# One order for the matrix memory of both sequences: scores turned on VectorE and through DRAM

## The chip, the cores and the metric

The kernel runs on one NeuronCore of a Trainium2 chip. The metric is the time of one execution on the device, in microseconds. The core has engines that each take their own instructions in order and wait for one another through semaphores: TensorE (PE, with its weight loads shown as PEld) for matmuls, VectorE (DVE), ScalarE (ACT), GpSimd (POOL) and SyncE (SP), which here only issues DMAs. An instruction that waits holds up everything behind it on its engine, and a DMA that waits holds up the DMAs issued behind it on the same queue.

## The reference

One layer of an encoder is applied to two sequences, `x_prompt` (below: the first, `s = 0`) and `x_sample` (the second, `s = 1`), of 512 tokens with 1024 channels each. Between two half-weighted feed-forward blocks stands a mix of two branches: grouped-query attention, and a bidirectional matrix memory with four heads of width 128.

```python
def encoder_layer(x, ...):
    x = x + 0.5 * swiglu(rms_norm(x, ffn1_norm), ...)
    h = rms_norm(x, mix_norm)
    proj = h @ w_in
    aq, ak, av, mq, mk, mv, gate_pre, o_pre, g_att, g_mlstm = jnp.split(proj, split_at, axis=-1)
    ...
    att = gqa_block_attention(aq, ak, av)
    mem = mlstm_bidirectional(mq, mk, mv, gate_pre, mlstm_gate_bias, o_pre, mlstm_head_norm)
    merged = jax.nn.sigmoid(g_att) * (att @ w_up_att) + jax.nn.sigmoid(g_mlstm) * (mem @ w_up_mlstm)
    x = x + merged @ w_out
    x = x + 0.5 * swiglu(rms_norm(x, ffn2_norm), ...)
    return x

def mlstm_bidirectional(q, k, v, gate_pre, ...):
    ...
    h = (h_fwd + h_bwd).transpose(0, 2, 1, 3)
    h = h * lax.rsqrt(jnp.mean(h * h, axis=-1, keepdims=True) + EPS)
    h = h.reshape(B, S, M_WIDTH) * head_norm
    return jax.nn.sigmoid(o_pre) * h

# inside one direction, for a chunk of 128 tokens:
        S_qk = jnp.einsum('bhtd,bhsd->bhts', qc, kc) * jnp.exp(D - m_t[..., None])
        num = jnp.einsum('bhts,bhse->bhte', S_qk, vc) + ...
        den = jnp.sum(S_qk, axis=-1) + ...
        h = num / jnp.maximum(jnp.abs(den), jnp.exp(-m_t))[..., None]
```

The kernel does not carry a state from chunk to chunk. For each head it forms the whole 512 x 512 matrix of decayed scores of both directions, divides its rows by the denominators, and multiplies it with the values.

## The kernel before, in words

**Precision and weights.** Every product is made of three matmuls, hi by hi, hi by lo and lo by hi, since each 32-bit operand is kept as a rounded high half and the remainder. The first sequence fetches a weight tile raw (L271, on SyncE, into a ring of four buffers with the tag `wr`), ScalarE makes the high half (L278), VectorE the low half (L279), both into a ring of four with the tag `w8`, and both halves are written to DRAM (`wpark`, L303). The second sequence reads them back from there already split (L293). `go(...)` takes units of work, each a load and a computation, and issues the load of a unit ahead of the computation of the unit before: one ahead in the first sequence, two in the second.

**The instruction order.** The text of the program gives each instruction a priority by its place; `shifted(n)` moves a piece forward or back. A scheduler at build time places instructions of each engine by their priority and by when their inputs are expected. So a change in the text's order, or of a ring from which a tile comes, can move instructions of all engines. In the stretches where `marks` is set, the matmuls at the ends of groups are pinned to the written order.

**The memory of one head** (inside `mix`):
- `mem_rows` (L1071, L1074): two DMAs on SyncE spread decay rows `ebuf` over the partitions into the tile `box` (a ring of four), and an addition with a mask makes a second copy of each. The masks of heads 1 to 3 of the first sequence are on GpSimd; all the others are on VectorE.
- `mem_head` (L1234 to L1281): four blocks of 128 rows of scores on TensorE (L1248, 12 matmuls of 512 columns); 20 exponentials on ScalarE (L1262); eight products with row sums on VectorE (L1264); the denominators (L1268 to L1270); and the two directions joined (L1275 on ScalarE, L1276 and L1278 on VectorE).
- The scores must be turned before they meet the values. The first sequence does that on TensorE in `mem_out`, with 16 transposes of 128 x 128 a head (L1307) into PSUM. The second one calls `mem_blocks` (L1283 to L1292) right behind `mem_head`: VectorE transposes within 32 x 32 blocks in eight instructions a head (L1286) into two `qt` tiles, taken from the ring `wr`; eight DMAs on SyncE (L1290) write them to `tbuf`, one of two DRAM buffers; and `mem_out` reads four blocks back by DMAs of GpSimd (L1303).
- `mem_out`: the turned block is split (L715 on ScalarE, L716 on VectorE), 12 matmuls with the values `Vm` follow (L1316), then the output gate (L1326) and the norm of the head: `block_sums` turns the squares on VectorE (L225) and reduces them (L226); `block_rstd` folds the sums with a small matmul (L232) and takes twelve operations on 128 x 16 numbers (L235 to L241); `spread_rows` (L258) and L1332 apply it, and the result is split into `mem`. Where the scores came through DRAM, the output is first copied into order by ScalarE (L1322).

**Units around it.** `mem_values` (L804, four units of 24 matmuls: `Vm`), `mem_qk` for heads 2 and 3, `att_gate`, `merge_att` (L839, L1215) and `mem_gate` are the units that give TensorE work while a head goes through ScalarE and VectorE. In the first sequence they are spread by a queue and `fill`; in the second one they are listed by hand between the heads.

The few lines that decide where the raw weights and the turned tiles live:

```python
        raw = wpool.tile(shape, F32, tag="wr", bufs=4, name=nm("wr"))                                            # L266
            q = [wpool.tile([P, 8, 4, 32], F32, tag="wr", bufs=4, name=nm("qt")) for _ in range(2)]              # L1283
```

Of the kernel before, what the change touches and what calls it, by code (L numbers as in the profile page):

```python
# [8 lines left out]
F32 = mybir.dt.float32  # L9
# [17 lines left out]
def encoder(ctx, tc, I, outs):  # L27
# [228 lines left out]
    def spread_rows(r16, R):  # L256

        nc.vector.transpose(R.rearrange("p (n j) -> p n j", j=32), r16.unsqueeze(2).to_broadcast([P, 16, 32]))  # L258
        return R
# [583 lines left out]
    FILLER = 5,3  # L843
    SOON = 7,1
    FIRST = 7,9,9,11
    EARLY = 6

    def mix(s, xh, xl, early=None, extra=None, after=None):

# [4 lines left out]
        def fill(n):  # L854
            go(*queue[:n])
            del queue[:n]
# [159 lines left out]
        def mem_qk(h, j):  # L1016
            def done(pp):
                if j == 0 and not s:
                    t = wpool.tile([P, 4, S], F32R, tag="w8", bufs=4, name=nm("qk"))
                    qks[h] = [t[:, i] for i in range(4)]  # L1020
                elif s:
                    t = mem[:, 2 + j] if h == 2 else wpool.tile([P, 2, S], F32R, tag="wr", bufs=4, name=nm("qk"))
                    qks.setdefault(h, []).extend(t[:, i] for i in range(2))
                t = pp
                if not s:
                    t = F2()
                    V_.tensor_tensor(t, pp, R[s], op=ALU.mult)
                split(t, *qks[h][2 * j:2 * j + 2])
            return win_cols((768, 1280)[j] + h * P, done)
# [264 lines left out]
        def mem_out(h, Ts):  # L1294
            moved = isinstance(Ts, int)
            vm = Vm[0]
            po = PO()
            hs_ = slice(h * P, (h + 1) * P)
            turned = []
            for j in range(4 + 1):  # L1300
                if j < 4 and moved:
                    p = F2()
                    nc.gpsimd.dma_start(p, tbuf[Ts][4 * j:4 * j + 4].rearrange("c r a x -> (c r) (a x)"))  # L1303
                elif j < 4:
                    p = PT()
                    for i in range(4):
                        nc.tensor.transpose(p[:, i * P:(i + 1) * P], Ts[i][0][:, j * P:(j + 1) * P], ident)  # L1307
                if j < 4:
                    ph, pl = T2(F32R), T2(F32R)
                    split(p, ph, pl)  # L1310
                    turned.append((j, ph, pl))
                if j >= 1:
                    t, ph, pl = turned.pop(0)
                    with shifted(15):
                        for n, (a, b) in enumerate(((0, ph), (1, ph), (0, pl))):
                            mark(nc.tensor.matmul(po, vm[:, a, t, hs_], b, start=(t == 0 and n == 0),  # L1316
                                                  stop=(t == 3 and n == 2)), True)
# [12 lines left out]
            with shifted(160):  # L1330
                Rh = spread_rows(rh, T2(F32, "f2"))
                V_.scalar_tensor_tensor(og, og, hn[:, h:h + 1], Rh, op0=ALU.mult, op1=ALU.mult)  # L1332
                split(og, mem[:, h, 0, :], mem[:, h, 1, :])

        if s:
            qk2, qk3 = [[mem_qk(h, j) for j in range(2)] for h in (2, 3)]
            ma = [merge_att(d) for d in range(KD)]
            marks[0] = True
            at = [mem_blocks(0, mem_head(0))]
            go(*mem_values(), *qk2)  # L1340
            at.append(mem_blocks(1, mem_head(1)))
            go(*qk3, ma[0], ma[1])
            mem_out(0, at[0])
            at.append(mem_blocks(2, mem_head(2)))
            go(att_gate(6), att_gate(7), ma[2], ma[3])
            mem_out(1, at[1])
            at.append(mem_blocks(3, mem_head(3)))
            go(*ma[4:])
            mem_out(2, at[2])
            go(*[mem_gate(d) for d in range(EARLY)])  # L1350
            mem_out(3, at[3])
            marks[0] = False
        for h in range(HM if not s else 0):
            Ts = mem_head(h)
            if h == 0:
                go(*mem_values())
            queue.append(merge_att(2 * h))
            if h == 0:
                queue.append(merge_att(1))
            fill(1 + s)  # L1360
            mem_out(h, Ts)
            if h + 2 < HM:
                queue.extend([att_gate(h + 6), mem_qk(h + 2, 0), mem_qk(h + 2, 1)])
            if h:
                queue.append(merge_att(2 * h + 1))
            fill(99)
# [543 lines left out]
```

## Time and profile before

| | us |
|---|---|
| runs | 2041.68, 2039.68, 2042.42 (median 2041.68) |
| profiled execution | 2039.86 |
| its span | 2038.1 |
| granted TensorE clock, mean | 0.999 |
| memory stage of the first sequence | about 800 to 980 of the span |
| memory stage of the second sequence | about 1180 to 1330 of the span |

The span is the stretch from the first to the last instruction that the profiler saw; the execution's own time is 1.8 us longer. In the lines that follow, a row of a timeline reads: start, duration, engine, line of the kernel, operation, what it writes and reads, and how many. "idle before" is the time for which that engine did nothing ahead of it, with what ended it. Matmuls are pipelined, so a single matmul's recorded duration is longer than the step from one to the next. Busy time on TensorE says that it is never without work, not that it works at its peak.

### The profile page before, as it was taken

The numbers are of one execution on the slowest core, as the hardware profiler recorded it, in microseconds if no ns is written. First come the engines' busy times: TensorE is split into PE (matmuls) and PEld (weight loads), VectorE is DVE, ScalarE is ACT, GpSimd is POOL, SyncE is SP. The second block draws the span as 40 slices with busy tenths as digits, with TensorE's granted clock in tenths as the row PEclk, the third lists the DMA queues.
The fourth block names the chain that finished last, engine by engine and source line by source line (L and its number), as shares of the span: only waits on it lengthen the run. The fifth ranks groups of instructions, "written<-read, shape, count | busy, mean of one in ns | idle before, by whom it ended". The sixth has DMA issues, their size and how long they took to land.

```text
span 2038.1 us, 26750 instructions
## 1 busy us (share of the span) xinstructions
PE 2026.7 (99%) x9249; PEld 1672.9 (82%) x9249; DVE 1580.7 (78%) x2812; ACT 912.3 (45%) x1659; POOL 101.2 (5%) x132
## 2 busy tenths in 40 slices
PE   9999999999999999999999999999999999999998
PEld 7888888888888888888888888788888888888887
DVE  8888888886797798776566767477788988786797
ACT  7644444442234577563324554235444444442224
POOL 0000000001003000100120000011000000000001
PEclk9999999999999999999999999999999999999999
DMA  9656566799766954868654367877565655699753
GB/s 320 197 167 220 178 209 189 238 334 365 268 214 224 292 176 135 274 212 294 199 186 141 110 191 241 272 231 231 180 197 175 212 171 177 205 347 345 272 197 119
DMA packets 324712, 453.78 MB, mean 223 GB/s; under 512 B 20616, under 2 KB 198880, under 8 KB 323296
## 3 DMA queue, kind: packets, MB, share of 16 engines
q1 hardware_dynamic: 321216, 441.89, 64.8%
q0 software_dynamic: 3200, 9.92, 1.5%
q8 instruction: 73, 1.20, 0.2%
q14 instruction: 63, 0.52, 0.1%
q10 hardware_dynamic: 160, 0.27, 0.0%
HBM read 288.25 MB, written 163.74 MB: 222 GB/s over the span
## 4 chain that ended last, share of the span: by engine, by line
PE 93%; DVE 3%; ACT 1%; DMA 1%; issue 1%; SPq 0%; POOL 0%; DVEq 0%; ACTq 0%; POOLq 0%
PE mm L839 13%; PE pso L374 12%; PE pst L374 12%; PE mm L374 10%; PE mm L632 9%; PE pss L374 6%; PE mm L825 5%; PE pss L632 4%; PE pst L632 4%; PE mm L804 4%; PE pso L632 3%; PE pso L1128 1%; PE pss L1101 1%; PE pst L1117 1%; PE pso L804 1%
## 5 line engine op out<-in xcount | busy, mean ns | idle before, releaser
L374 PE MATMUL pst<-xc,w 128*128 128x512 f32 x1056 | 253.7, 389 | 0.0
L374 PEld LDWEIGHTS pst<-xc,w 128*128 128x128 f32 x1056 | 198.2, 188 | 41.1
L374 PE MATMUL mm<-xc,w 128*128 128x512 f32 x972 | 229.7, 390 | 0.3 <-ACT f L382 0.3
L374 PEld LDWEIGHTS mm<-xc,w 128*128 128x128 f32 x972 | 181.9, 188 | 38.4 <-ACT f L382 0.7
L632 PE MATMUL mm<-rt,w 128*128 128x512 f32 x765 | 178.7, 389 | 0.0
L839 PE MATMUL mm<-xh,w 128*128 128x512 f32 x560 | 176.2, 391 | 0.0
L632 PEld LDWEIGHTS mm<-rt,w 128*128 128x128 f32 x765 | 143.6, 188 | 29.7
L332 ACT ACTIVATE w<-t 128x512 fp32r<-128x512 f32 x176 | 106.5, 627 | 135.7 <-issue 63.1
L333 DVE TENSOR_TENSOR w<-t,w 128x512 fp32r<-128x512 f32 x176 | 117.6, 686 | 45.7 <-ACT w L332 44.1
L374 PE MATMUL pso<-xc,f 128*128 128x512 f32 x528 | 127.0, 389 | 0.0
L374 PE MATMUL pss<-xc,w 128*128 128x512 f32 x528 | 126.8, 389 | 0.0
L374 PE MATMUL pso<-xc,w 128*128 128x512 f32 x528 | 126.8, 389 | 0.0
L839 PEld LDWEIGHTS mm<-xh,w 128*128 128x128 f32 x560 | 104.9, 188 | 21.9
L374 PEld LDWEIGHTS pso<-xc,f 128*128 128x128 f32 x528 | 99.0, 188 | 20.9 <-DVE t L413 0.4
L374 PEld LDWEIGHTS pso<-xc,w 128*128 128x128 f32 x528 | 99.1, 188 | 20.6
L374 PEld LDWEIGHTS pss<-xc,w 128*128 128x128 f32 x528 | 99.1, 188 | 20.6
L825 PE MATMUL mm<-xh,w 128*128 128x512 f32 x336 | 113.4, 400 | 0.0
L839 PE MATMUL mm<-xl,w 128*128 128x512 f32 x280 | 109.6, 391 | 0.0
L715 ACT ACTIVATE w<-wr 128x512 fp32r<-128x512 f32 x72 | 45.1, 632 | 137.0 <-PE pso L632 65.1
L279 DVE TENSOR_TENSOR w<-wr,w 128x1024 fp32r<-128x1024 f32 (+1 forms) x64 | 79.7, 1246 | 27.5 <-ACT w L278 15.6
L278 ACT ACTIVATE w<-wr 128x1024 fp32r<-128x1024 f32 (+1 forms) x64 | 65.3, 1029 | 79.5 <-issue 24.5
L715 ACT ACTIVATE w<-t 128x512 fp32r<-128x512 f32 x82 | 51.8, 632 | 107.4 <-PE pst L632 62.4
(455 smaller groups left out, 4068.9 us busy)
## 6 DMA issues: line engine op xcount, KB each, us to landing
rt<-rbuf SPq DMA_DIRECT2D x154, 512.0 KB, 5.7
wpark<-w SPq DMA_DIRECT2D x88, 512.0 KB, 3.9
w<-wpark SPq DMA_DIRECT2D x88, 512.0 KB, 5.1
wr<-in_ffn_w_gate_dram SPq DMA_DIRECT2D x62, 512.0 KB, 5.3
rbuf<-tab SPq DMA_DIRECT2D x102, 256.0 KB, 4.0
wr<-in_ffn_w_up_dram SPq DMA_DIRECT2D x44, 512.0 KB, 4.6
rbuf<-f SPq DMA_DIRECT2D x72, 256.0 KB, 4.0
wr<-in_w_in_dram SPq DMA_DIRECT2D x36, 512.0 KB, 6.1
```

Of the source, the lines that this page charges most:

```text
L278: pin(nc.scalar.activation(hi, raw, AF.Copy))
L279: pin(lo_eng.tensor_tensor(lo, raw, f(hi), op=ALU.subtract))
L332: pin(nc.scalar.activation(t[:, 0], src, AF.Copy))
L333: pin(V_.tensor_tensor(t[:, 1], src, f(t[:, 0]), op=ALU.subtract))
L374: nc.tensor.matmul(p, a[:, k, :], xt[:, b, k, :], start=(first and k == 0 and i == 0), stop=(k == HK_ - 1 and i == 2), skip_group_check=True)
L632: nc.tensor.matmul(p, u[:, a, d * P:(d + 1) * P], r[:, b, ts], start=(first and q == 0 and k == 0), stop=(q == len(us) - 1 and k == 2), sk ...
L715: nc.scalar.activation(hi, src, AF.Copy)
L804: mark(nc.tensor.matmul(p[b][:, :N], a[:, k, bs], w_[:, kl, :], start=(k == 0 and i == 0), stop=(k == KD - 1 and i == 2)), (kl, b, i) == ( ...
L825: pin(nc.tensor.matmul(p[0], a[:, k, :], b, start=(k == 0 and i == 0), stop=(k == n - 1 and i == 2)))
L839: mark(nc.tensor.matmul(p, a[:, k, :], b, start=(k == 0 and i == 0), stop=last), last)
L1101: pin(nc.tensor.matmul(p, qT[:, h, b * P:(b + 1) * P], kv[:, hk * 2 + j, :], start=(j == 0), stop=(j == 1)))
L1117: pin(nc.tensor.transpose(p[:, b * P:(b + 1) * P], Ps[b][:, kb * P:(kb + 1) * P], ident))
```

## The change

The first sequence now takes the way of the second one. `mem_blocks` follows `mem_head` for each head, and `mem_out` reads the turned blocks from DRAM; the transposes on TensorE aren't called any more. The units around the heads stand in one list for both sequences, and a table `STEPS` says how many of them are issued behind each `mem_blocks` and behind each `mem_out`; `until(n)` counts the units that `go` holds back. The pins of `marks` now hold in the first sequence too. In the norm of a head the squares' transpose and the spread of the result use the same tile.

```diff
-    def block_sums(t, tag="f2"):
+    def block_sums(t, q=None):
...
-        q = T2(F32, tag)
+        q = T2(F32, "f2") if q is None else q
...
-    EARLY = 6
+    STEPS = (4, 4), (8, 8), (12, 12), (16, 22)
...
-            row = block_sums(h2)
+            turned_ = F2()
+            row = block_sums(h2, turned_)
...
-                Rh = spread_rows(rh, T2(F32, "f2"))
+                Rh = spread_rows(rh, turned_)
...
-        if s:
-            qk2, qk3 = [[mem_qk(h, j) for j in range(2)] for h in (2, 3)]
-            ma = [merge_att(d) for d in range(KD)]
-            marks[0] = True
-            at = [mem_blocks(0, mem_head(0))]
-            go(*mem_values(), *qk2)
-            at.append(mem_blocks(1, mem_head(1)))
-            go(*qk3, ma[0], ma[1])
-            mem_out(0, at[0])
...
-            mem_out(3, at[3])
-            marks[0] = False
-        for h in range(HM if not s else 0):
-            Ts = mem_head(h)
-            if h == 0:
-                go(*mem_values())
-            queue.append(merge_att(2 * h))
-            if h == 0:
-                queue.append(merge_att(1))
-            fill(1 + s)
-            mem_out(h, Ts)
...
+        qk2, qk3 = [[mem_qk(h, j) for j in range(2)] for h in (2, 3)]
+        ma = [merge_att(d) for d in range(KD)]
+        late = [*mem_values(), *qk2, *qk3, *ma[:2], att_gate(6), att_gate(7), *ma[2:],
+                *[mem_gate(d) for d in range(KD)]]
+
+        def until(n):
+
+            n += ahead[0] - len(late_at)
+            late_at.extend(range(max(n, 0)))
+            go(*[late.pop(0) for _ in range(max(n, 0))])
+
+        late_at = []
+        marks[0] = True
+        at = []
+        for h, (before, behind) in enumerate(STEPS):
+            at.append(mem_blocks(h, mem_head(h)))
+            until(before)
+            if h:
+                mem_out(h - 1, at[h - 1])
+            until(behind)
+        mem_out(HM - 1, at[HM - 1])
+        marks[0] = False
...
-        go(*[mem_gate(d) for d in range(EARLY * s, KD)])
+        go(*late)
```

Three places show how instructions move. The numbers behind a name only tell tiles apart. The first is the queue of SyncE at the end of the first sequence's attention. `wr` are raw weights, `wpark` the split ones on their way to DRAM; the four tiles `wr_7039`, `wr_7047`, `wr_7083` and `wr_7115` of before are those of `mem_values`, as are `wr_7057`, `wr_7065`, `wr_7101` and `wr_7133` now. Before:

```order
L303 DMA wpark_6327<-w_6324 128x1024 x2
L271 DMA wr_7039<-in_w_in_dram 128x2x512
L303 DMA wpark_6433<-w_6430 128x1024 x2
L271 DMA wr_7047<-in_w_in_dram 128x2x512
L303 DMA wpark_6545<-w_6542 128x1024 x2
L271 DMA wr_7083<-in_w_in_dram 128x2x512
L303 DMA wpark_6657<-w_6654 128x1024 x2
L271 DMA wr_7115<-in_w_in_dram 128x2x512
L303 DMA wpark_7044<-w_7041 128x1024 x2
L271 DMA wr_7147<-in_w_up_att_dram 128x4x256
L303 DMA wpark_7052<-w_7049 128x1024 x2
L271 DMA wr_7277<-in_w_in_dram 128x8x128
```

And of the change:

```order
L303 DMA wpark_6327<-w_6324 128x1024 x2
L303 DMA wpark_6433<-w_6430 128x1024 x2
L303 DMA wpark_6545<-w_6542 128x1024 x2
L303 DMA wpark_6657<-w_6654 128x1024 x2
L1071 DMA box_5276<-ebuf_5283 128x4x128 x2
L271 DMA wr_7057<-in_w_in_dram 128x2x512
L271 DMA wr_7065<-in_w_in_dram 128x2x512
L1290 DMA tbuf_259<-qt_7039 32x8x128 x4
L1290 DMA tbuf_259<-qt_7040 32x8x128 x4
L303 DMA wpark_7062<-w_7059 128x1024 x2
L303 DMA wpark_7070<-w_7067 128x1024 x2
L271 DMA wr_7101<-in_w_in_dram 128x2x512
```

The raw weights of `mem_values` moved from between the `wpark` writes to behind the two `ebuf` loads of head 1, and the third and fourth stand behind the writes of head 0's turned tiles as well.

The second is TensorE at the end of the attention: L1128 is the attention's output, L1248 the scores of the memory, L804 `mem_values`. Before, where `mem_values` runs between the rows of the attention:

```order
L804 MATMUL mm_7056<-w_7041,xh_4896 128x512 x2
L804 MATMUL mm_7056<-w_7041,xl_4897 128x512
L804 MATMUL mm_7057<-w_7041,xh_4896 128x512
L1248 MATMUL pss_6973<-qk_5678 128x512 x2
L1128 MATMUL pso_6853<-t_695_6870,kv_5277 128x512
L1248 MATMUL pss_6973<-qk_5678 128x512
L804 MATMUL mm_7057<-w_7041,xh_4896 128x512
L804 MATMUL mm_7057<-w_7041,xl_4897 128x512
L1128 MATMUL pso_6853<-t_696_6871,kv_5277 128x512
```

And of the change, from the last row of the attention on:

```order
L1128 MATMUL pso_6920<-t_717_6940,kv_5277 128x512
L1248 MATMUL pss_6999<-qk_5678 128x512 x3
L1248 MATMUL pss_7012<-qk_5678 128x512 x3
L1248 MATMUL pss_7211<-qk_5817 128x512 x3
L1248 MATMUL pss_7224<-qk_5817 128x512 x3
L1248 MATMUL pss_7237<-qk_5817 128x512 x2
L804 MATMUL mm_7073<-w_7059,xh_4896 128x512
L804 MATMUL mm_7074<-w_7059,xh_4896 128x512
L804 MATMUL mm_7075<-w_7059,xh_4896 128x512
```

No row of `mem_values` stands inside the attention any more; the scores of head 1 (`qk_5817`) come before its first one.

The third is VectorE around head 2. L1264 to L1278 are the head's products, denominators and sums, L279 the low half of a weight that TensorE takes soon after. Before:

```order
L1264 SCALAR_TENSOR_TENSOR t_849_7727,dn_7683<-pss_7723,t_849_7727 128x512
L1264 SCALAR_TENSOR_TENSOR t_850_7733,dn_7683<-pss_7723,t_850_7733 128x128
L1215 SCALAR_TENSOR_TENSOR mg_5281<-mg_5281,mm_7758 128x512
L1268 SCALAR_TENSOR_TENSOR dn_7683<-dn_7683 128x8
L279 TENSOR_TENSOR w_7934<-wr_7932,w_7934 128x1024
L1269 TENSOR_TENSOR dn_7683<-dn_7683,st_5284 128x8
L279 TENSOR_TENSOR w_8047<-wr_8045,w_8047 128x1024
L1270 RECIPROCAL dn_7683<-dn_7683 128x8
```

And of the change, where the head's block transposes end:

```order
L1286 STREAM_TRANSPOSE qt_7580<-t_818_7544 128x8x32
L1286 STREAM_TRANSPOSE qt_7581<-t_818_7544 128x8x32
L1286 STREAM_TRANSPOSE qt_7580<-t_821_7557 128x8x32
L1286 STREAM_TRANSPOSE qt_7581<-t_821_7557 128x8x32
L258 STREAM_TRANSPOSE f_807_7487<-row_7488 128x512
L716 TENSOR_TENSOR t_844_7714<-f_842_7711,t_843_7713 128x512
L1333 SCALAR_TENSOR_TENSOR box_5276<-box_5276,hn,f_807_7487 128x512
L716 TENSOR_TENSOR t_847_7723<-f_845_7720,t_846_7722 128x512
L279 TENSOR_TENSOR w_7614<-wr_7612,w_7614 128x1024
L716 TENSOR_TENSOR mem_6967<-box_5276,mem_6967 128x512
L279 TENSOR_TENSOR w_7636<-wr_7634,w_7636 128x1024
```

Where weights were split in the middle of a head's work, the first one (`w_7614`) now stands behind all of head 2's work and behind the norm of head 0 (L258, L1333), which is 47 instructions behind that norm's first one (L1326). TensorE's row for that weight, a product for `att_gate(6)`, comes right behind the first scores of head 3. From one kernel to the other all line numbers below 1326 are the same; L1333 is the L1332 of before.

More of the change, by code (lines that the diff above doesn't have):

```diff
@@ L1330, in mem_out @@
             with shifted(160):
-                Rh = spread_rows(rh, T2(F32, "f2"))
+                Rh = spread_rows(rh, turned_)
                 V_.scalar_tensor_tensor(og, og, hn[:, h:h + 1], Rh, op0=ALU.mult, op1=ALU.mult)
                 split(og, mem[:, h, 0, :], mem[:, h, 1, :])
-        if s:
-            qk2, qk3 = [[mem_qk(h, j) for j in range(2)] for h in (2, 3)]
-            ma = [merge_att(d) for d in range(KD)]
-            marks[0] = True
-            at = [mem_blocks(0, mem_head(0))]
-            go(*mem_values(), *qk2)
-            at.append(mem_blocks(1, mem_head(1)))
-            go(*qk3, ma[0], ma[1])
-            mem_out(0, at[0])
[L1344 to L1350, printed above, removed]
-            mem_out(3, at[3])
-            marks[0] = False
@@ L1353, in mix @@
-        for h in range(HM if not s else 0):
-            Ts = mem_head(h)
-            if h == 0:
-                go(*mem_values())
-            queue.append(merge_att(2 * h))
-            if h == 0:
-                queue.append(merge_att(1))
-            fill(1 + s)
-            mem_out(h, Ts)
-            if h + 2 < HM:
-                queue.extend([att_gate(h + 6), mem_qk(h + 2, 0), mem_qk(h + 2, 1)])
+        qk2, qk3 = [[mem_qk(h, j) for j in range(2)] for h in (2, 3)]
+        ma = [merge_att(d) for d in range(KD)]
@@ L1364, in mix @@
             if h:
-                queue.append(merge_att(2 * h + 1))
-            fill(99)
+                mem_out(h - 1, at[h - 1])
+            until(behind)
+        mem_out(HM - 1, at[HM - 1])
+        marks[0] = False
         mh, ml = A([P, KD, S], F32R, "mh"), A([P, KD, S], F32R, "ml")
-        go(*[mem_gate(d) for d in range(EARLY * s, KD)])
+        go(*late)
         go(*[merge_mem(d) for d in range(KD)])
```

## The prediction

> **What bounds the kernel now.** I read the page first: busy shares, then the chain of work that ended last.
>
> ```profile
> span 2038.1 us, 26750 instructions
> ...
> PE 2026.7 (99%) x9249; PEld 1672.9 (82%) x9249; DVE 1580.7 (78%) x2812; ACT 912.3 (45%) x1659; POOL 101.2 (5%) x132
> ...
> PE 93%; DVE 3%; ACT 1%; DMA 1%; issue 1%; SPq 0%; POOL 0%; DVEq 0%; ACTq 0%; POOLq 0%
> ```
>
> TensorE is busy for 2026.7 of 2038.1 us and 93% of the chain is its own work. So time comes off only if TensorE loses work, and goes on as soon as TensorE is made to wait. VectorE at 78% looks roomy, but that is an average. The table of busy time by stretch shows the memory stage of the first sequence (three rows) and that of the second, which already turns its scores on VectorE (last row); columns are the stretch, its length, then busy time and count of TensorE, its weight loads, VectorE, ScalarE, GpSimd, the granted clock, the DMA share and GB/s.
>
> ```profile
> 810.00:820.00 10.00, 10.00 (x46) 8.00 (x45) 7.65 (x21) 9.64 (x26) 0.00 (x0) 1.00 0.17 51
> 820.00:830.00 10.00, 10.00 (x46) 8.28 (x45) 6.73 (x14) 4.86 (x8) 1.71 (x1) 1.00 0.93 370
> 860.00:870.00 10.00, 10.00 (x53) 7.93 (x52) 8.37 (x18) 5.60 (x11) 0.00 (x0) 1.00 1.02 342
> 1260.00:1280.00 20.00, 19.01 (x84) 15.29 (x84) 16.86 (x56) 8.83 (x23) 1.61 (x3) 1.00 0.75 241
> ```
>
> TensorE has no hole in the first sequence's stage. In the second's it idles about 1 us in twenty, with VectorE at 84%. The cover is there, but in the first sequence VectorE and ScalarE also have to split every raw weight, which in the second come out of DRAM already split.
>
> **What is removed.** Sixty-four transposes on TensorE (L1307), four for each of 16 blocks. The group, then TensorE's timeline (start, duration, engine, line, count):
>
> ```profile
> L1307 PE MATMUL pst<-ident,t 128*128 128x128 f32 x64 | 9.7, 275 | 0.0
> ```
>
> ```profile
> 833.93 0.60 PE L1307 MATMUL pst<-ident,t 128*128 128x128 f32 x4
> 834.29 0.48 PE L1316 MATMUL pso<-t,Vm 128*128 128x512 f32 x1
> 834.61 0.60 PE L1307 MATMUL pst<-ident,t 128*128 128x128 f32 x4
> 834.96 1.41 PE L1316 MATMUL pso<-t,Vm 128*128 128x512 f32 x5
> 836.20 0.85 PE L839 MATMUL mm<-att,w 128*128 128x512 f32 x3
> ...
> 837.86 3.81 PE L839 MATMUL mm<-att,w 128*128 128x512 f32 x16
> 841.51 0.39 PE L839 MATMUL mm<-xh,w 128*128 128x512 f32 x1
> ```
>
> Sixteen 512-wide matmuls take 841.51 - 837.86 = 3.65 us, 0.228 each. From 833.93 to 836.20 are 2.27 us for six matmuls (1.37) and eight transposes, so 0.9 / 8 = 0.1125 us each. The group's 275 ns is a pipelined record, not a price. 64 x 0.1125 = **7.2 us** off TensorE.
>
> **What is added and hidden.** Thirty-two block transposes on VectorE, 32 DMA writes, 16 reads and four ScalarE copies (one a head); in return one f2 tile a head fewer. The second sequence shows the transposes:
>
> ```profile
> 1195.86 2.07 DVE L1286 STREAM_TRANSPOSE qt<-t 128x256 f32<-128x256 f32 x6
> PE pso L1316 <- ACT t L715: 1.0, 1, 1.0
> ```
>
> 2.07 / 6 = 0.34 us each, 2.75 us a head. The second row, TensorE's waits there, is the whole price of the route in the second sequence: 1.0 us on the turned scores. The head norm's single tile I cost at nothing: turn and spread follow each other on VectorE in any case; cover gone, it would be one 0.7 us operation a head, bounds 0 to 2.8 us.
>
> **What is moved: the first weights of the memory's values.** The new listing shows the cost that the diff hides. The `qt` tiles come from the same four-buffer ring as the raw weights. In SyncE's queue the first two weight loads of mem_values now stand behind both ebuf loads of head 1. Those wait until ScalarE has read head 0's copies, which already is SyncE's longest wait here. SyncE and GpSimd, then ScalarE, then the ends of TensorE's runs, from the timelines; after them the loads' minimum, median and maximum from issue to landing (L271):
>
> ```profile
> SPq L1071 <- ACT t L1262: 11.9, 1, 11.9
> 804.59 0.43 SPq L271 DMA_DIRECT2D wr<-in_w_in_dram  x1
> 816.68 0.37 SPq L1071 DMA_DIRECT2D box<-ebuf  x1
> 821.01 1.71 POOL L1074 TENSOR_TENSOR box<-box,tab 128x512 f32<-128x512 f32 x1 [159.25 <-DMA wpark<-w]
> ```
>
> ```profile
> 815.09 1.85 ACT L1262 ACTIVATE t<-box,st 128x128 f32<-128x128 f32 x6
> 817.80 1.56 ACT L1262 ACTIVATE t<-box,st 128x128 f32<-128x128 f32 x5
> 819.26 1.05 ACT L278 ACTIVATE w<-wr 128x1024 fp32r<-128x1024 f32 x1
> 821.71 1.92 ACT L1275 ACTIVATE t<-t,dn 128x128 f32<-128x128 f32 x4
> ```
>
> ```profile
> 798.90 0.71 PE L804 MATMUL mm<-w,xh 128*128 128x512 f32 x2
> 812.19 0.39 PE L1128 MATMUL pso<-t,kv 128*128 128x512 f32 x1
> 831.11 0.40 PE L804 MATMUL pso<-w,xl 128*128 128x512 f32 x1
> ```
>
> ```profile
> DMA to landing us min/median/max: 4.7/5.4/6.3
> ```
>
> Before, mem_values starts at 798.90, fills the waits of the attention's tail (19 matmuls before 812.4, 19 x 0.228 = 4.3 us) and ends at 831.34. Now step by step: the tail ends near 811.9; head 0's exps end at about 817.7 (before 819.05, with one split of 1.04 between them that is now gone); the second ebuf load is issued then, lands 4.3 later (816.68 to 821.01), 822.1; GpSimd's mask takes 1.5 (rows 1.3 to 1.7), 823.6; the split of the first weight stands on ScalarE behind 12 of head 1's exps, 12 x 0.31 = 3.75 (1.56 / 5), 827.4; the split 1.05, 828.5. The weight itself, issued behind the ebuf loads, lands by about 824, so it is not last. From 811.9 TensorE has 14 score matmuls, 3.2 us, so it idles **about 13.4**. It waits 0.5 for the low half; 48 matmuls run to 840.0, the four left of head 1's scores to 840.9. The third weight's high half stands on ScalarE behind L1275 (1.9), which waits for VectorE's last four L1264 (1.8) and the denominators (0.6); with the split of 1.0 that gives 845.8, **4.9** idle. Its low half stands behind four block transposes (1.35) and its own 1.15: **1.2** more. 48 matmuls end mem_values at 857.9. Against 831.34 it ends 26.6 late, and the 12 matmuls of head 1's scores (2.7) are done early: **23.9 us** lost.
>
> **Heads 2 and 3.** Before, the low halves of weights (L279) stand inside a head's VectorE work. Now head 2's whole work and head 0's norm stand in front of the next weight's. VectorE's groups and timeline:
>
> ```profile
> L1264 DVE SCALAR_TENSOR_TENSOR t<-pss,t 128x128 f32<-128x128 f32 (+3 forms) x32 | 14.6, 485 | 1.9 <-ACT t L1262 1.1 <-PE pss L1248 0.7
> ```
>
> ```profile
> 844.00 0.17 DVE L235 TENSOR_SCALAR row<-pst 128x16 f32<-128x16 f32 x1
> ...
> 846.50 0.71 DVE L258 STREAM_TRANSPOSE f<-row 128x512 f32<-128x512 f32 x1
> 847.24 0.75 DVE L1332 SCALAR_TENSOR_TENSOR box<-box,hn,f 128x512 f32<-128x512 f32 x1
> ...
> 860.93 0.68 DVE L1278 TENSOR_SCALAR t<-t,dn 128x384 f32<-128x384 f32 x2
> ...
> 862.25 0.68 DVE L1027 TENSOR_TENSOR f<-mm,R 128x512 f32<-128x512 f32 x1
> 862.85 0.60 DVE L1276 SCALAR_TENSOR_TENSOR t<-t,dn,t 128x128 f32<-128x128 f32 x2
> 863.84 1.23 DVE L279 TENSOR_TENSOR w<-wr,w 128x1024 fp32r<-128x1024 f32 x1 [0.38 <-ACT w L278]
> 864.98 0.69 DVE L716 TENSOR_TENSOR qk<-f,qk 128x512 fp32r<-128x512 f32 x1
> ```
>
> A 512-wide operation costs 0.60 start to start (862.25 to 862.85). The queue: eight L1264, 8 x 14.6 / 32 = 3.6; seven L1276 and L1278, 1.3 + 0.6 = 1.9; eight block transposes 2.75; five wide operations of the norm 3.1; its twelve row operations 2.5 (844.00 to 846.50); three splits and one L1215 2.4; three on the denominators 0.6; the weight 1.15 (863.84 to 864.98). Sum **18.0 us**, starting 0.7 after the last output matmul (one 0.6 ScalarE copy). TensorE has 24 matmuls and the fold, 5.7, and two that need only the high half, 0.5: idle 18.7 - 6.2 = **12.5**. Head 3 has 19.9 of queue (two more splits, one more L279) against 33 matmuls, 7.5: **about 12.8**. Behind mem_out(2) ScalarE's split for the first memory gate stands behind head 2's norm and split: 24 matmuls and the fold, then 2.5 + 0.7 + 0.7 of the norm, 0.6 and 1.05 on ScalarE and 1.15 for the low half: **6.75**. Small waits (a late low half 1.45, mem_out(0) 0.2) add 1.7.
>
> **Sum.** 23.9 + 12.5 + 12.8 + 6.75 + 1.7 = 57.6 us of new idle, less 7.2: +50.4. The profiled execution took 2039.86; 2090.3. It is 1.8 under the median of the runs, so I say **2091**.
>
> **Bounds.** The first 23.9 rests on an issue order and hard waits: 20 to 27 with a landing of 4.7 to 6.3. The rest rests on VectorE's queue being taken in order with nothing to spare: at least 0, where the scores' waits run as in the second sequence (1.0 us in all), and at most about 40, where the turned blocks also come back late.
>
> A point where a rule speaks: after a standstill TensorE may be slow. The start of the trace:
>
> ```profile
> 1.63 2.93 PE L1398 MATMUL pst<-xc 128*128 128x512 f32 x6 [1.63 <-DVE xc L1482]
> ```
>
> Six matmuls from rest take 2.93 us, 0.49 each against 0.228. The Trainium skill ("TensorE: Matmul & The Clock Gate", "HAM oscillation — how this bites in real kernels") says that gaps above about 3.4 us drop the array to half clock until it has been busy again. The row agrees in size, though the granted clock is shown as full there; no gap inside the kernel is that long, so nothing here shows the drop after one. Half of some 3.4 us, an estimate from that page, would be 1.7 us for each of six gaps, 10 us in all.
>
> **Rivals.**
> - *The transposes were pure TensorE time and everything else stays covered.* For it: the second sequence does so with 1.0 us of waits. Against: SyncE's 11.9 us wait now stands in front of raw weights. It decides if the first weight lands and is split before 812, so is issued before about 805. Time 2039.9 - 7.2 = 2033. Chance 0.06.
> - *The losses are about as large as the gain*, because only the tail's 4.3 and some 3 us of waits come: 2040. Chance 0.03.
> - *Only the first gap.* Weights for heads 2 and 3 are split early enough since TensorE is already late and VectorE catches up: 2039.9 - 7.2 + 23.9 + 1.7 = 2058. Against: VectorE's program order, 47 operations before that weight. Chance 0.15.
> - *The forecast, with matmuls slow after each gap.* From the start's row, 6 x 0.26 = 1.6 us a gap, for six gaps 9.6: 2101. For: that row; against: the clock shown there is full. The skill's rule gives the same 2101. Chance 0.14.
> - *The forecast*: 2075 to 2105, likeliest 2091. Chance 0.62.
>
> **How the numbers follow.** The first two cases, 0.09 together, are left out of the range. It begins at 2056, just under the third case's 2058, and ends at 2110, which takes in the fourth case's 2101 and the longer landings and late blocks of the bounds; what may lie above it and below it I put at another 0.1. Faster is the first rival's 0.06, no change the second's 0.03, slower the rest, 0.91. Some 0.2%, 4 us, is about what a measurement of this kernel can tell from no change.
>
> **What would show it.** TensorE idle for about 13 us between 812 and 828, in one or two pieces, waiting for ScalarE's L278; two gaps of some 12 us ended by L279; one of 6 to 7 ended by L278; no L804 before 820; the L1307 group gone; busy TensorE time down by 7. I am wrong if L804 runs in the attention's tail, if the gaps at heads 2 and 3 are short, or if VectorE finishes its head queue in less than 12 us.

## The result, and the profile after

The changed kernel takes 2098.53 us (median of four runs, 2097.88 to 2099.42) against 2041.97 us before: a ratio of 1.0284, 95% interval 1.0270 to 1.0297, so 57 us slower. The profiled execution took 2097.88 us.

The page of the changed kernel, to be read against the first lines of the prediction:

```profile
span 2096.1 us, 26756 instructions
...
PE 2039.0 (97%) x9185; PEld 1675.6 (80%) x9185; DVE 1595.1 (76%) x2844; ACT 916.4 (44%) x1663; POOL 111.3 (5%) x148
...
PE 91%; DVE 5%; DMA 1%; ACT 1%; issue 1%; SPq 0%; DVEq 0%; ACTq 0%
```

TensorE has 64 instructions fewer (9249 to 9185), yet is busy 12.3 us longer, and the chain goes through VectorE more than before (5% against 3%). TensorE's waits in the memory stage of the first sequence (window 780 to 1060, from the view of waits; the columns are the total, how often, and the longest), where before there were none at all:

```profile
PE mm L839 <- ACT w L278: 14.2, 3, 6.2
PE pss L1248 <- DVE t L1264: 11.7, 8, 7.2
PE mm L839 <- DVE w L279: 9.1, 4, 4.0
PE mm L804 <- ACT w L278: 5.1, 2, 4.7
PE pst L232 <- DVE row L226: 3.1, 2, 2.9
```

L278 and L279 are the two halves of a weight. The same stage as one row of the table by stretch, first of the kernel before, then of the changed one:

```profile
790.00:1050.00 260.00, 259.99 (x1244) 214.83 (x1243) 186.64 (x395) 128.35 (x253) 22.51 (x27) 1.00 0.68 223
```

```profile
790.00:1050.00 260.00, 213.89 (x894) 167.01 (x893) 164.19 (x344) 109.31 (x214) 25.36 (x28) 0.89 0.69 222
```

So 46.1 us of idle on TensorE where there was 0.01, and a granted clock of 0.89 where it was 1.00. The gaps one by one, in TensorE's timeline of the changed kernel:

```profile
813.91 1.19 PE L1248 MATMUL pss<-qk 128*128 128x512 f32 x3 [2.14 <-DVE t L1264]
815.46 2.82 PE L1248 MATMUL pss<-qk 128*128 128x512 f32 x6 [0.35 <-DVE t L1264]
...
826.59 1.22 PE L1248 MATMUL pss<-qk 128*128 128x512 f32 x2 [7.19 <-DVE t L1264]
828.24 2.07 PE L804 MATMUL mm<-w,xh 128*128 128x512 f32 x4 [0.43 <-ACT w L278]
...
846.56 1.65 PE L804 MATMUL mm<-w,xh 128*128 128x512 f32 x3 [4.69 <-ACT w L278]
...
860.25 0.39 PE L804 MATMUL pso<-w,xl 128*128 128x512 f32 x1
...
884.03 1.52 PE L1248 MATMUL pss<-qk 128*128 128x512 f32 x6
...
905.65 0.79 PE L839 MATMUL mm<-xh,w 128*128 128x512 f32 x1 [5.32 <-ACT w L278]
...
910.87 1.22 PE L839 MATMUL mm<-xh,w 128*128 128x512 f32 x2 [4.00 <-DVE w L279]
...
930.07 0.40 PE L232 MATMUL pst<-row,fold 128*128 128x16 f32 x2 [2.94 <-DVE row L226]
...
968.46 0.80 PE L839 MATMUL mm<-xh,w 128*128 128x512 f32 x1 [6.18 <-ACT w L278]
```

The first matmul of mem_values runs at 828.24, where it ran at 798.90. And the row at 815.46 shows the second loss: six score matmuls take 2.82 us there, while six of the same kind take 1.52 us at 884.03. The table by stretch has the granted clock for the first of them (third value from the end):

```profile
814.50:817.75 3.25, 2.90 (x7) 1.64 (x6) 2.15 (x8) 3.23 (x12) 0.00 (x0) 0.50 0.13 37
```

Behind a gap TensorE works at half speed for a while; that is how it can be busy longer with less work. Busy time rose by 12.3 us with an estimated 7.2 us of work gone, so TensorE's own work took up to about 19.5 us longer. The granted clock accounts for most of that: multiplied with the busy time in stretches of half a microsecond, from 790 to 990, what it falls short of full speed comes to 16.8 us. The rest is not shown to be the clock; the recorded end of a pipelined matmul ahead of each gap counts as busy too. The span grew by 58.0 us: 45.7 of idle time, which is this stage's, and 12.3 of busy time.

### The profile page after: what moved, and what is told of

Read it like the earlier page. It is cut to its first block, busy times and chain, and to the rows that moved or that the text cites. A ratio compares the mean times of both kernels' runs of the same rounds, so it can differ in the third digit from the quotient of the medians.

```text
span 2096.1 us, 26756 instructions
## 1 busy us (share of the span) xinstructions
PE 2039.0 (97%) x9185; PEld 1675.6 (80%) x9185; DVE 1595.1 (76%) x2844; ACT 916.4 (44%) x1663; POOL 111.3 (5%) x148
## 4 chain that ended last, share of the span: by engine, by line
PE 91%; DVE 5%; DMA 1%; ACT 1%; issue 1%; SPq 0%; DVEq 0%; ACTq 0%
PE mm L839 15%; PE pso L374 11%; PE pst L374 11%; PE mm L374 11%; PE mm L632 8%; PE pss L374 6%; PE mm L825 5%; PE pss L632 4%; PE pst L632 4%; PE mm L804 3%; PE pso L632 3%; PE pso L1128 1%; PE pss L1101 1%; PE pst L1117 1%; PE pso L1316 1%; PE pso L804 1%
## 5 line engine op out<-in xcount | busy, mean ns | idle before, releaser
L839 PE MATMUL mm<-xh,w 128*128 128x512 f32 x560 | 180.8, 401 | 17.0 <-ACT w L278 11.5
L825 PE MATMUL mm<-xh,w 128*128 128x512 f32 x336 | 113.4, 400 | 0.0
L715 ACT ACTIVATE w<-wr 128x512 fp32r<-128x512 f32 x72 | 45.1, 632 | 137.1 <-PE pso L632 70.7
L715 ACT ACTIVATE w<-t 128x512 fp32r<-128x512 f32 x82 | 51.8, 632 | 107.4 <-PE pst L632 62.4
L279 DVE TENSOR_TENSOR w<-wr,w 128x1024 fp32r<-128x1024 f32 (+1 forms) x64 | 79.6, 1249 | 23.2 <-ACT w L278 12.5
L632 PE MATMUL pss<-rt,w 128*128 128x512 f32 x396 | 93.7, 389 | 0.0
```

The costliest lines, as they stand in the source:

```text
L279: pin(lo_eng.tensor_tensor(lo, raw, f(hi), op=ALU.subtract))
L632: nc.tensor.matmul(p, u[:, a, d * P:(d + 1) * P], r[:, b, ts], start=(first and q == 0 and k == 0), stop=(q == len(us) - 1 and k == 2), sk ...
L715: nc.scalar.activation(hi, src, AF.Copy)
L825: pin(nc.tensor.matmul(p[0], a[:, k, :], b, start=(k == 0 and i == 0), stop=(k == n - 1 and i == 2)))
L839: mark(nc.tensor.matmul(p, a[:, k, :], b, start=(k == 0 and i == 0), stop=last), last)
```

## The experiments

The theory after this reading (theory 1): TensorE starves because raw weights are fetched and split behind the memory's own work. Rivals: the route through VectorE and DRAM is late in any order (A); the number of units per step or the pins are wrong (B); and, from the fifth experiment on, VectorE and ScalarE have no room at heads 1 to 3 (C). Each ratio is against runs of the kernel before on the same chip.

**Units ahead of the turning.** The first experiment moves one line:

```diff
-            at.append(mem_blocks(h, mem_head(h)))
-            until(before)
+            Ts = mem_head(h)
+            until(before)
+            at.append(mem_blocks(h, Ts))
```

> The changed kernel, but behind each head's scores the next units (weights included) are written ahead of the block transposes instead of behind them. Nothing else differs: same route through DRAM, same table of steps, same pins. Theory 1 (TensorE starves because raw weights are fetched and split behind the memory's own work): the loads of mem_values come early again, mem_values fills the attention's tail, the first gap (about 25 us with its slow clock) goes and the gaps at heads 2 and 3 shrink, so 2035 to 2065. Rival A (the route is the cost: VectorE's turns and the trip through DRAM come back late in any order): stays above 2085. Rival B (the number of units per step, or the pins, is wrong): about 2098, since neither is touched.

2064.22 us, ratio 1.0118 (1.0104 to 1.0132). The place of one call in the text is worth 34 of the 57 us. Its waits in the same window:

```profile
PE mm L839 <- ACT w L278: 15.6, 4, 6.2
PE mm L839 <- DVE w L279: 3.7, 2, 2.8
PE pso L1316 <- ACT t L715: 1.5, 1, 1.5
```

Every wait before 838 is gone (the first one ends at 840.77), and those for L1264 with them. What stays are waits for weights at heads 1 to 3. The turned blocks themselves (L715) cost 1.5 us: rival A is out as the main cause, and so is B, since counts and pins are those of the change.

**Only the first weights early.**

```diff
+            if not s and h == 0:
+                until(before)
             at.append(mem_blocks(h, mem_head(h)))
```

> The changed kernel, but the units of mem_values are written before head 0's scores; heads 1 to 3 stand as in the changed kernel. Theory 1: only the first gap goes, about 25 us of it, and the gaps at heads 2 and 3 stay: 2068 to 2080, with TensorE still idle around L232, L278 and L279 at heads 2 and 3. Rival A: 2090 or more. Rival B: about 2098.

2092.51 us, ratio 1.0255 (1.0239 to 1.0271): a miss. The first gap is gone, but nearly all of it came back a head later. SyncE and TensorE in its timeline:

```profile
841.36 0.37 SPq L1071 DMA_DIRECT2D box<-ebuf  x1
841.83 12.90 SPq L1290 DMA_DIRECT2D tbuf<-qt  x16
854.77 2.33 SPq L271 DMA_DIRECT2D wr<-in_w_in_dram  x3
```

```profile
860.22 0.79 PE L839 MATMUL mm<-xh,w 128*128 128x512 f32 x1 [16.79 <-ACT w L278]
```

Three weight loads stand behind the sixteen tbuf writes of heads 0 and 1, which wait for VectorE. So the first gap was not a loss of the start alone: here the weights that follow come after the whole next head, and taking the gap out at head 0 gained only 6 us.

**The old order with the new route.** In the kernel before, the loop of the first sequence calls mem_blocks:

```diff
-            Ts = mem_head(h)
+            Ts = mem_blocks(h, mem_head(h))
```

> The kernel before, with its own order of units for the first sequence, but with mem_blocks behind mem_head there too, so that its scores go through VectorE and DRAM. No table of steps, no pins in the first sequence. Theory 1: qt tiles still come out of the weights' ring ahead of the values' weights, so the first gap is there, and heads 2 and 3, whose units keep their old places, lose less: 2050 to 2080. Rival A: as the changed kernel, about 2098. Rival B: the old order is good, so the transposes' 7.2 us show: about 2035.

2104.77 us, ratio 1.0313 (1.0299 to 1.0327), slower than the change. So the table of steps isn't the cause: the old order of units with the new route loses even more. Theory 1 had expected 2050 to 2080 and was wrong in size again. The run before suggests why, but no run shows it for this order.

**The head norm alone.** The kernel before with `turned_` as in the diff:

```diff
-            row = block_sums(h2)
+            turned_ = F2()
+            row = block_sums(h2, turned_)
```

> The kernel before, with the head norm's turn and spread in one f2 tile and nothing else. All theories: 2039 to 2044, no difference that can be told (0 to 2.8 us by the prediction).

2037.77 us (11 runs), ratio 0.9984 (0.9975 to 0.9993): 2.9 us faster, a small gain, and the only version here that beats the kernel before. The expectation, 2039 to 2044, was missed by little; I had weighed the edit as a possible cost only. Why it gains was not looked into.

**The tiles out of the weights' ring, in three kernels.** The turned tiles of the first sequence go into the four ebuf slots of `box` (with the order of the change, with the old order, and with units first):

```diff
-            q = [wpool.tile([P, 8, 4, 32], F32, tag="wr", bufs=4, name=nm("qt")) for _ in range(2)]
+            q = [wpool.tile([P, 8, 4, 32], F32, tag="wr", bufs=4, name=nm("qt")) if s else
+                 boxes["tile"][:, 2 * g:2 * g + 2, :]... for g in range(2)]
```

> The changed kernel, with the first sequence's two qt tiles in the four ebuf slots of box (free once a head's exponentials are read) and no longer in the ring of raw weights. Order of units, pins, route and counts as in the changed kernel. Theory 1, now narrowed to the ring (each head's qt tiles take two of four raw-weight buffers until VectorE has turned the head and SyncE has written it, so every following weight is fetched and split late): almost all of the loss goes at all heads, 2032 to 2050, though the next head's ebuf loads now wait for the tbuf writes. Rival C (VectorE and ScalarE have no room at heads 1 to 3, whatever the buffers): 2070 or more. Rival A (the route returns late): 2080 or more.

2069.49 us, ratio 1.0139 (1.0124 to 1.0154). Nothing but the home of two tiles changed in the text, and half of the loss went. But not almost all, as theory 1 had it (2032 to 2050). Its waits:

```profile
PE pss L1248 <- DVE t L1264: 11.4, 4, 4.6
PE pso L1317 <- ACT t L715: 5.6, 2, 5.3
PE pst L232 <- DVE row L226: 2.8, 1, 2.8
PE mm L839 <- DVE w L279: 1.7, 1, 1.7
```

Waits for weights fell to 1.7 us. In their place TensorE waits for scores and turned blocks. The next head's ebuf loads now stand behind the tbuf writes: those of head 1 are issued at 830.31 instead of 816.00, and GpSimd's masks start at 836.84 instead of 819.82. That is the new wait that the expectation named, and I had priced it too low.

> The kernel before with the new route in the first sequence (as in the run with the old order), and the qt tiles in the ebuf slots of box. Theory 1 as narrowed: the 62 us of loss of that run go too, since they came from the same ring: 2032 to 2055. Rival C: 2070 or more. Rival B (the order of units): between 2032 and 2050 here but not with the table of steps.

2081.56 us, ratio 1.0196 (1.0179 to 1.0213): 23 us better than with the ring, far from the 2032 to 2055 of theory 1. One wait of 20.2 us for a turned block (L715), up to 960.22, appeared: in the old order a head's blocks are read back right behind its own turning, and here SyncE issues their writes only at 949.40.

> Both edits: units written ahead of the block transposes, and the qt tiles in the ebuf slots of box. Theory 1 as narrowed: the ring was the only cause, so this adds little to the run with box alone, within 8 us of it. If the place in the text counts by itself, it is faster by 10 us or more. Rival C: no gain over the run with weights first, 2064.

2065.39 us, ratio 1.0119 (1.0104 to 1.0134): the same as with units first alone, 2064.22, and within the 8 us of 2069.49 that theory 1 allowed. But the waits are others:

```profile
PE pso L1317 <- ACT t L715: 5.8, 4, 1.6
PE pss L1248 <- DVE t L1264: 4.5, 3, 3.3
PE mm L839 <- ACT w L278: 2.5, 2, 2.3
```

Waits for weights (L278 and L279) come to 3.6 us here and to 19.3 with units first alone, while those for scores and turned blocks come to 11.1 here and to 1.5 there. Each edit takes out most of the same loss, and together they gain no more than units first alone; but the equal times hide different remainders and don't show that ring and place in the text are one cause.

**What a gap costs.** In the kernel before, two standstills among the first sequence's memory gates. The small transposes and the copies add work that the reference doesn't have, and in this stretch every matmul is pinned to the written order:

```diff
-        return pin(i) if last and marks[0] else i
+        return pin(i) if (last and marks[0]) or marks[0] == 2 else i
...
+                if not s and d in GAPS:      # GAPS = {1: 1, 4: 8}
+                    a = T2()
+                    for _ in range(GAPS[d]):
+                        nc.scalar.activation(a, t if _ == 0 else a, AF.Copy)
+                    pin(nc.tensor.transpose(PO()[:, 0:P], a[:, 0:P], ident))
...
+        marks[0] = 2 * (1 - s)
         go(*[mem_gate(d) for d in range(EARLY * s, KD)])
```

> The kernel before with two forced standstills of TensorE among the first sequence's memory gates: a small transpose that waits for one ScalarE copy (a gap of some 2.2 us) and, three units later, one that waits for eight (some 6.5 us). It measures what a gap costs beyond its own length. If gaps cost only their length: 2040.7 + 9 = about 2050, and matmuls step at 0.228 us right after both. If a gap over about 3.4 us lowers the clock: matmuls step near 0.43 us for several us behind the long gap and not behind the short one, 2052 to 2055.

2056.08 us, ratio 1.0076 (1.0061 to 1.0091): 15.3 us for gaps of 2.88 and 6.96 us. TensorE's timeline behind each, then four rows of the table by stretch, in which the granted clock is the third value from the end:

```profile
928.18 0.47 PE L1228 MATMUL pso<-ident,t 128*128 128x128 f32 x1 [2.88 <-ACT t L1227]
928.31 0.78 PE L839 MATMUL mm<-xh,w 128*128 128x512 f32 x1
...
930.59 0.91 PE L839 MATMUL mm<-xh,w 128*128 128x512 f32 x2
931.33 0.39 PE L839 MATMUL mm<-xl,w 128*128 128x512 f32 x1
...
953.20 0.47 PE L1228 MATMUL pso<-ident,t 128*128 128x128 f32 x1 [6.96 <-ACT t L1227]
953.33 0.78 PE L839 MATMUL mm<-xh,w 128*128 128x512 f32 x1
...
958.17 0.78 PE L839 MATMUL mm<-xh,w 128*128 128x512 f32 x2
```

```profile
926.00:930.00 4.00, 1.82 (x5) 1.54 (x6) 3.37 (x12) 2.09 (x3) 0.00 (x0) 0.72 1.13 359
...
927.75:931.00 3.25, 2.82 (x7) 2.27 (x8) 2.88 (x9) 0.47 (x2) 0.00 (x0) 0.50 1.03 351
...
954.00:958.00 4.00, 4.00 (x11) 3.14 (x10) 0.00 (x0) 0.00 (x0) 0.00 (x0) 0.50 0.01 2
...
962.00:966.00 4.00, 4.00 (x19) 3.33 (x18) 1.45 (x2) 1.11 (x2) 0.00 (x0) 1.00 0.64 262
```

Behind the long gap 11 matmuls take 958.17 - 953.33 = 4.84 us, 0.44 each, at a granted clock of 0.50; with 0.228 each they would take 2.5. Behind the short gap seven take 931.33 - 928.31 = 3.02 us, and 1.6 at 0.228. So the long gap cost some 2.3 us beyond its length and the short one some 1.4. That the short one lowers the clock too was not expected. The gaps and these two add up to 13.5. The rest of the 15.3 is not shown to belong to the clock; in that run the second sequence also waited 2.3 us longer for its turned blocks than before.

**The tiles in the scores' ring.** The turned blocks in four 128 x 512 tiles of the `t2` ring, two at a time, with 16 writes a head instead of 8, so that neither weights nor ebuf loads wait for a buffer:

```diff
+            if not s:
+                for k in range(2):
+                    q = [T2().rearrange("p (n i m) -> p n i m", i=2, m=32) for _ in range(2)]
+                    ...
+                                dma_start(tbuf[h % 2][8 * g:8 * g + 8, :, a, 64 * k:64 * k + 64]...)
+                return h % 2
```

> The changed kernel, with the first sequence's turned blocks in four 128x512 tiles of the ring that the scores use (two at a time, each freed by its writes) instead of two of the weights' four buffers; 16 DMA writes of half the row length a head instead of 8. Here neither the raw weights nor the next head's ebuf loads wait for the turning. Theory 1 as narrowed: this is what is left when the ring alone is taken away, 2032 to 2045, with raw weights loaded as early as in the kernel before. Rival C (no room on VectorE and ScalarE at heads 1 to 3): 2055 or more, with TensorE waiting for L1264 or L715 rather than for weights.

2072.54 us, ratio 1.0148 (1.0131 to 1.0165). Theory 1 had 2032 to 2045. The ring is out of the way and TensorE has no gap over 0.5 us before 846. Then it waits 8.3 us for a weight at 858.57. SyncE's timeline shows that weight's load behind the writes of the turned blocks again, this time without any shared buffer:

```profile
842.72 7.89 SPq L1292 DMA_DIRECT2D tbuf<-t  x16
850.71 0.90 SPq L303 DMA_DIRECT2D wpark<-w  x2
851.65 2.27 SPq L271 DMA_DIRECT2D wr<-in_w_in_dram  x2
```

> As the run before, with units written ahead of the block transposes as well. Theory 1 as narrowed: within 6 us of the run before. Rival C: no gain over 2064 of the run with weights first.

2072.53 us, ratio 1.0155 (1.0140 to 1.0171): as the run before, though slower than units first with the ring, 2064. Here TensorE waits 11.4 us for L1264 and 15.8 for L278. Why it is slower with more buffers is left open.

**The waiting DMAs on another queue.** The tbuf writes and the ebuf loads of heads 1 to 3 are issued by GpSimd in the first sequence:

```diff
-                    nc.sync.dma_start(tbuf[h % 2][8 * g:8 * g + 8, ...
+                    (nc.sync if s else nc.gpsimd).dma_start(tbuf[h % 2][8 * g:8 * g + 8, ...
-            nc.sync.dma_start(eb3, ...
+            (nc.sync if s or not h else nc.gpsimd).dma_start(eb3, ...
```

> The changed kernel, with the first sequence's tbuf writes and the ebuf loads of its heads 1 to 3 issued by GpSimd instead of SyncE. The qt tiles stay in the weights' ring. Two causes are still mixed: the ring (two of four raw-weight buffers are held until a head is turned and written) and SyncE's queue (DMAs that wait for VectorE or ScalarE stand in front of weight loads). If the queue is the larger part, 2050 to 2075 here and the first gap shrinks, since the first two weights no longer stand behind the ebuf loads. If the ring is the larger part, 2080 or more.

2102.27 us, ratio 1.0301 (1.0286 to 1.0317): no gain. So moving the waiting DMAs off SyncE's queue frees nothing by itself. That the buffers keep the loads late wherever the writes are issued fits this, but is not shown: the waits moved to GpSimd's queue, which stood up to 24.4 us for a head's turning ahead of the tbuf writes.

> Both: units written ahead of the block transposes, and those DMAs on GpSimd. The ring gives weights their buffers first, and no weight load stands behind a DMA that waits for a head. If ring and queue are the whole cause, 2032 to 2048, the fastest with this route. Rival C (no room on VectorE and ScalarE): 2055 or more, with TensorE waiting for L1264 or for L715 of the turned blocks and not for weights.

2059.79 us, ratio 1.0094 (1.0078 to 1.0111), the best with the new route, and still slower than before. Its waits:

```profile
PE mm L839 <- ACT w L278: 5.6, 1, 5.6
PE pso L1316 <- ACT t L715: 5.1, 2, 3.5
PE pso L1316 <- DVE t L716: 4.1, 2, 2.5
PE pss L1248 <- DVE t L1264: 1.1, 1, 1.1
```

One wait of 5.6 us for a weight is left: ScalarE had waited 15.35 us for its load. The turned blocks (L715, L716) now cost 9.2 us. In this profiled execution, 2056.57 us, TensorE's idle in the stage is 18.2 us, and the slow clock over its busy time, worked out as above, about 5.0; less the 7.2 this is 16.0 of the 16.7 us above the kernel before. In four runs theory 1 had almost the whole loss go, 2055 at the highest, and missed all of them (2069, 2082, 2073 and 2060); the least times of rival C for them were met in three and missed by 0.5 us in one. So rivals A and C are not the cause of most of the 57 us, but the remainder fits C as well as theory 1, and no run decides between them.

## Why the prediction was right, point by point

The time, 2098.53, lies in the range, 7.5 us above the predicted 2091 and 2.5 below the fourth rival's 2101; of the cases it is the forecast's mechanism joined with that of this rival, the slow matmuls behind gaps. The path was right: weights that are fetched and split behind the memory's own work. The number is partly luck, since two errors of size nearly cancel.

- **What is removed.** Sixty-four instructions, as said. Their 7.2 us can't be seen by themselves in any run here, since no arrangement kept TensorE covered; they stay an estimate.
- **The first weights.** The chain of steps came out nearly as written: first matmul of mem_values forecast at 828.5, seen at 828.24; the third weight at 845.8, seen at 846.56; the end of mem_values at 857.9, seen at 860.5. What TensorE waited for was read less well: of some 10.3 us idle between 811.9 and 828.24, 9.8 were ended by L1264, as the scores of head 1 were held up too, and 0.43 by L278. The weight's high half, which ScalarE ended at 828.2, would have held mem_values back until then all the same. The rows of SyncE and GpSimd in the changed kernel are the ones that the steps named:

```profile
816.00 1.54 SPq L1071 DMA_DIRECT2D box<-ebuf  x2
817.60 1.01 SPq L271 DMA_DIRECT2D wr<-in_w_in_dram  x2
825.43 3.95 SPq L1290 DMA_DIRECT2D tbuf<-qt  x8
```

```profile
822.33 1.26 POOL L1074 TENSOR_TENSOR box<-box,tab 128x512 f32<-128x512 f32 x1 [1.20 <-DMA box<-ebuf]
```

- **Heads 2 and 3.** VectorE's queue at head 2 was priced at 18.0 us; it ran from about 892.1 (L1326, one 0.6 us operation ahead of the L225 at 892.75) to the end of the weight's low half at 910.73, 18.6 us. The idle there was forecast at 12.5 and is 11.3 (the two large gaps, 5.32 and 4.00, and 2.0 in small ones). The first of the two ended with the weight's high half, for whose load ScalarE itself had waited 1.16 us, and only the second with the low half. At head 3, 12.8 became about 9.5; the last one, 6.75, is 6.18.
- **Two sums of the working** don't come out as stated, and neither matters. Landings of 4.7 to 6.3 us in place of 4.3 give 24.3 to 25.9 for the first weights, not 20 to 27; and head 3's terms give 19.9 + 0.7 - 7.5 = 13.1, not 12.8.
- **The norm's single tile** was put at nothing, with a cost of up to 2.8 us as its bound. Alone it gains 2.9, so the sign was wrong.
- **The sum of idle time** was 57.6 and is 46.1. Part of the difference is not a mistake about the weights: while TensorE waits, its own matmuls run at half speed and fill some of the wait. The 14 score matmuls ahead of mem_values, priced at 3.2 us, took 6.2 by their records (1.19, 2.82, 0.96 and 1.22); some of that is the pipelined end of each record and not the clock.
- **The term that was mis-sized** is the one left at nothing: the clock behind gaps. The forecast counted a gap at its own length and kept the slow clock as a rival at 1.6 us for each of six gaps, 9.6 in all, with a chance of 0.14. It measured 16.8 by the granted clock and up to 19.5 by busy time, at a granted clock of 0.89 over the stage. The two errors, 11.5 us too much idle and 17 to 19.5 too little for slow work, nearly cancel. The rule that was weighed, that of the Trainium skill ("TensorE: Matmul & The Clock Gate", "HAM oscillation — how this bites in real kernels"), drops TensorE to half clock behind gaps above about 3.4 us. These runs agree on the half clock (0.50 from 954 to 958, behind 6.96 us) but not on the bound: recorded gaps of 2.88 us, and of 2.14 with smaller waits ahead of it, were enough (last section).
- **What would show it.** Some of the signs named appeared: no L804 before 820, the L1307 group gone, a gap of 6.18 ended by L278, and 18.6 us for VectorE's queue. Others did not. Between 812 and 828 it was some 10 us and not 13, with nearly all of it ended by L1264 and not by L278. There were no two gaps of 12 us ended by L279: the longest that it ended was 4.00, and head 3 had only pieces below 3. Busy TensorE time was said to fall by 7 and rose by 12; that is, for the most part, the clock again.

What the runs add to the reasons: the larger part of the loss comes from the units' weights standing behind the block transposes of each head (34 us for one line moved). The shared ring is worth 29 undone alone, and nothing more on top of that line. Both edits change the order of the instructions too, so a buffer that is held and an instruction that comes late are not told apart. Taken out at head 0 alone it comes back at the next head. What stays open is the remainder, 19 us in the best version with the new route and about 24 to 40 in the others without the ring: waits for weights, for scores and for turned blocks and the clock are all in it, in other shares each time, and no run separates them.

## What to carry to other kernels

A long-lived tile that is taken from a ring of prefetch buffers can make everything that the ring serves come later (29 us here): put the consumer's long-lived tile elsewhere, or ask for the prefetches first, and look at the DMA queue's order before counting the work that is saved. Where a route is copied from a stretch in which weights come ready-made to one in which they are still split by the same engines, the cover is not copied with it. In these runs a standstill of TensorE cost its length and a piece of half-speed work behind it (some 1.4 us behind 2.88, 2.3 behind 6.96), so several middling gaps are dearer than their sum.

## What the hardware showed that was not expected

The clock fell behind a recorded gap of 2.88 us: the granted clock was 0.72 over the four microseconds from 926, and five matmuls behind it took 0.46 us each instead of 0.228. Only two small matmuls of the norm and the added transpose stand between the last full-width matmul ahead, which starts at 924.41, and the first behind, at 928.31, so by full-width work the standstill is longer than 2.88. In the changed kernel six matmuls behind a gap of 2.14 us took 2.82 us instead of 1.52, though TensorE had also been waiting in smaller pieces before that. Both times the granted clock was at half for about 3.4 us: from 927.8 to 931.2 and from 814.5 to 817.9, in the second case only after the matmuls had started again at 813.91. In the kernel before, with one wait of 1.0 us in the second sequence's memory, the granted clock stayed at 1.00.
